# Twelve weight slots, an earlier second x block, TensorE fillers and transposed sums in the opening of a two-layer hybrid backbone

## The chip, the cores and the metric

The kernel runs on one core of one Trainium2 chip. The metric is the device time of one execution in microseconds (us). TensorE (PE) multiplies matrices, VectorE (DVE), ScalarE (ACT) and GpSimd (POOL) do the elementwise work, and SyncE (SP) issues most of the DMA transfers from one queue, in order. Every engine works through its own queue in order and waits on semaphores for the others.

## The reference, cut to what matters

There are 1024 latent tokens and 256 context tokens of width 1024 and two layers. Each layer first makes six vectors of modulation from the conditioning, one set for the latent and one for the context tokens, and normalises:

```python
mod   = jax.nn.silu(c)     @ w_mod[l] + b_mod[l]      # (1, 3072): shift, scale, gate
mod_c = jax.nn.silu(c_ctx) @ w_mod[l] + b_mod[l]
h  = rms_norm(x, norm_g[l]) * (1.0 + scale)   + shift
hc = rms_norm(y, norm_g[l]) * (1.0 + scale_c) + shift_c
pl, pc = split_cols(h @ w_in[l]), split_cols(hc @ w_in[l])
o  = concat(attention(pl, pc), gated_delta_net(pl, pc), rg_lru(pl, pc)) @ w_out[l]
x  = x + gate * o
```

The three mixers read the same projection. The output is a last RMSNorm of x.

## The kernel before

Data is held transposed, 128 features by tokens. The tokens come in three blocks: A and B are the two halves of the latent tokens (512 each) and C the context (256). A normalised block h has eight parts d = 0 to 7 of 128 features each. The product with w_in is done in 34 tiles of 128 output columns; every tile does 24 matmuls for each block, since every operand is split into a high and a low part in fp32r (hi·hi, hi·lo, lo·hi for each d). The weights of a tile are loaded to "raw", rounded by ACT to "whi" (L841), and DVE makes "wlo" (L846).

The order of every engine's queue is not written by hand. A planner (class `Driver`) runs threads that yield operations with an estimated cost, and picks the one with the least start time plus priority; the priorities (`PR` and, for the second layer, `PR1`), the order of the tiles (`ORDER`, `ORDER1`) and some penalties are tables of numbers. So a change of one estimate can move instructions everywhere.

The opening, up to the third tile, runs in this way:

- Small constants are loaded by SP. Then `x_load` (L807) loads block A of x in eight parts, and `mod_load` (L635) the modulation weights: 4 chunks of 4 loads of 512 KB, in the order of chunks 0, 2, 1, 3. Chunks 0 and 2 hold shift and scale of d = 0 to 3, chunks 1 and 3 those of d = 4 to 7. The weights go to four slots "modw" of region X and to a buffer "sys" of region Y that takes two; a slot is free again when TensorE has used it. Blocks B and C of x are loaded after chunk 3.
- `mod_thread` (L658) multiplies a chunk with the vector silu(c) (tile "sc"), four matmuls side by side in 32 columns of the array each. ACT copies the sums out (L679), four small matmuls with the constant "sel2" add the four strips and transpose them (`fin`), and DVE adds the bias (L687) to modT; after a scale chunk it makes scA (L694).
- `stats` (L704) squares the parts (ACT L717), adds them up on DVE and POOL (L711), sums over partitions by a matmul with "ones", and makes the factor rs by two ACT steps (L733, L735). `norm_h` (L738) then multiplies each part by rs (L754), waits for the modulation of its half, scales and shifts it (L779), rounds it on ACT (L781) and makes the low part (L759, on DVE or POOL). After every four parts TensorE multiplies them with "wba" (`gates`); ACT copies that out (L792), TensorE transposes it with "sel16", and DVE copies it to "ba" (L802).
- `inproj` runs the first two tiles part by part, as the parts of h come; only when both are complete for A, B and C does it start the third tile.

Later in layer 0 an attention tile holds one of two locks from its start until its rotary step is done, and the table "rope" of that step is loaded after the DeltaNet inverses. The modulation of the gates and of layer 1 (eight more chunks, with the same `fin`) is made beside the attention.

Of the kernel before, what the change touches and what calls it, by code (L numbers as in the profile page):

```python
# [25 lines left out]
GROUPS = ((2, 3, 4, 5), (6, 7, 8, 9), (0, 1))  # L26

# [194 lines left out]
class Driver:  # L222


    def __init__(self):
# [7 lines left out]
        self.PR = {"att": -2.4, "att_k": -1.32, "att_q": -12.72, "atth": 0.74, "ba": 1.17, "evac": 0.39,  # L233
                   "gchain": 0.89, "gdn_q": -1.49, "gdn_v": 0.21, "gfin": -3.27, "gprep": 0.9, "gside": 1.09,
                   "inproj": 1.19, "inv": 1.02, "lru_x": -0.06, "lru_z": -2.13, "modlate": -1.36, "modload":
                   -14.53, "norm": -1.22, "normA": -8.86, "normB": -12.46, "normC": -3.27, "oproj": 0.33,
                   "osplit": -1.07, "prep": -1.73, "ptev": -0.13, "resid": -0.33, "rope": -1.03, "score": -0.15,
                   "wprep": -1.16, "z": -0.5}
        self.ops, self.late = [], False
        self.PR1 = {"att": -1.6, "att_k": -11.15, "att_q": -0.84, "atth": 0.05, "ba": -0.18, "evac": 0.37,  # L240
                    "gchain": 1.49, "gdn_q": -4.86, "gdn_v": 0.29, "gfin": -0.21, "gprep": 0.77, "gside": 0.4,
                    "inproj": 0.8, "inv": 0.24, "lru_x": -0.55, "lru_z": -0.49, "normA": 1.08, "normB": -1.62,
                    "normC": 12.1, "oproj": -1.07, "osplit": -0.26, "prep": -2.77, "ptev": -10.13, "resid":
                    -16.91, "rope": 3.42, "score": -0.66, "wprep": 1.03, "z": -0.87}
        self.margin, self.setpen, self.tilepen = 2.83, 1.1, 0.27
        self.cap = {"pe": 0.54, "dve": 0.3, "act": 0.26, "pool": 0.41}
# [209 lines left out]
def layout(inp):  # L456
# [57 lines left out]
    s2 = np.zeros((128, 2), np.float32)  # L514
    for j in range(4):
        for i in range(2):
            s2[32 * j + i, i] = 1.0
    A["sel2"] = s2
# [10 lines left out]
class Build:  # L529
# [1752 lines left out]
```

## Time and profile before

| | us |
|---|---|
| median of 3 runs | 2031.7 (2027.27 to 2031.89) |
| profiled execution, its own time | 2025.07 |
| its span | 2023.4 |
| TensorE busy in the span | 1927.2 (95%) |
| mean granted TensorE clock | 0.977 of full speed |

The profile's page gives for each engine the busy time, and in a band of 40 slices the busy tenths. TensorE is busy nearly everywhere; the exceptions are the first two slices, the end, and a few places in between. Matmuls are pipelined and their ends are modelled, so "busy" is not the same as "at its peak". The granted clock (PEclk) is 1.00 at 2.4 GHz and 0.50 at 1.2 GHz.

### The profile page before, as it was taken

The numbers are of one execution on the slowest core, as the hardware profiler recorded it, in microseconds if no ns is written. First come the engines' busy times: TensorE is split into PE (matmuls) and PEld (weight loads), VectorE is DVE, ScalarE is ACT, GpSimd is POOL, SyncE is SP. The second block draws the span as 40 slices with busy tenths as digits, with TensorE's granted clock in tenths as the row PEclk, the third lists the DMA queues.
The fourth block names the chain that finished last, engine by engine and source line by source line (L and its number), as shares of the span: only waits on it lengthen the run. The fifth ranks groups of instructions, "written<-read, shape, count | busy, mean of one in ns | idle before, by whom it ended". The sixth has DMA issues, their size and how long they took to land.

```text
span 2023.4 us, 34895 instructions
## 1 busy us (share of the span) xinstructions
PE 1927.2 (95%) x13014; PEld 1538.9 (76%) x13014; DVE 1321.9 (65%) x2556; ACT 1061.3 (52%) x1895; POOL 424.3 (21%) x604
## 2 busy tenths in 40 slices
PE   5899999999999999999999999999998999999997
PEld 2578888877888876777888688877776898776785
DVE  4767777898744356685533768969898444777433
ACT  3477676567333245465422577765667332566432
POOL 1402020000145522100331211110000676100132
PEclk8899999999999889999999999999999999899998
DMA  8037562325487868564633046563343888534643
GB/s 296 25 108 206 154 190 81 100 71 165 142 282 251 266 228 267 171 196 148 224 125 128 34 132 194 163 174 83 86 165 131 270 254 270 195 95 138 204 148 123
DMA packets 311738, 338.01 MB, mean 167 GB/s; under 512 B 63136, under 2 KB 220432, under 8 KB 311568
## 3 DMA queue, kind: packets, MB, share of 16 engines
q1 hardware_dynamic: 291696, 321.10, 51.1%
q10 hardware_dynamic: 19872, 14.68, 2.2%
q8 instruction: 102, 1.67, 0.4%
q14 instruction: 68, 0.56, 0.1%
HBM read 235.58 MB, written 94.87 MB: 163 GB/s over the span
## 4 chain that ended last, share of the span: by engine, by line
PE 65%; DVE 14%; ACT 8%; DMA 7%; issue 4%; SPq 1%; POOL 1%; ACTq 0%; DVEq 0%; POOLq 0%
PE psum L568 61%; PE psum L2017 3%; DVE regy L1317 3%; DVE regy L779 1%; DVE regy L577 1%; ACT regx L1950 1%; DVE regy L754 1%; DMA regy<-in_wmod_dram 1%; DVE wlo L846 1%; DVE regy L1479 1%; ACT whi L841 1%; DMA regy<-regy 1%; DVE regy L1324 1%; DVE regy L1481 1%; PE psum L1199 1%
## 5 line engine op out<-in xcount | busy, mean ns | idle before, releaser
L568 PE MATMUL psum<-regx,whi 128*128 128x512 f32 (+1 forms) x3328 | 953.2, 372 | 18.9 <-ACT regy L1224 8.9
L568 PEld LDWEIGHTS psum<-regx,whi 128*128 128x128 f32 x3328 | 592.2, 189 | 145.5 <-issue 19.6
L568 PE MATMUL psum<-regx,wlo 128*128 128x512 f32 (+1 forms) x1664 | 610.6, 367 | 0.4 <-DVE wlo L846 0.4
L568 PEld LDWEIGHTS psum<-regx,wlo 128*128 128x128 f32 x1664 | 314.8, 189 | 53.6 <-DVE wlo L846 0.8
L568 PE MATMUL psum<-regy,regy 128*128 128x128 f32 (+4 forms) x4064 | 318.9, 265 | 6.9 <-DMA regy<-regy 4.7
L568 PEld LDWEIGHTS psum<-regy,regy 128*128 128x128 f32 (+2 forms) x4064 | 265.7, 148 | 53.6 <-issue 28.1
L841 ACT ACTIVATE whi<-raw 128x1024 fp32r<-128x1024 f32 (+1 forms) x132 | 125.7, 953 | 171.8 <-PE psum L568 159.6
L568 PE MATMUL psum<-regx,regx 128*64 128x256 f32 (+2 forms) x1184 | 195.4, 368 | 5.3 <-DVE regx L1916 1.6
L846 DVE TENSOR_TENSOR wlo<-raw,whi 128x1024 fp32r<-128x1024 f32 (+1 forms) x100 | 117.5, 1176 | 69.0 <-ACT whi L841 67.2
L568 PE MATMUL psum<-regy,whi 128*128 128x512 f32 (+1 forms) x576 | 157.9, 360 | 4.5 <-DVE regy L2090 2.3
L568 PEld LDWEIGHTS psum<-regx,regx 128*128 128x128 f32 (+1 forms) x1184 | 116.0, 166 | 56.1 <-issue 26.3
L846 POOL TENSOR_TENSOR wlo<-raw,whi 128x768 fp32r<-128x768 f32 x32 | 59.1, 1847 | 347.6 <-ACT whi L841 309.4
L1224 ACT ACTIVATE regy<-psum 128x512 f32<-128x512 f32 (+1 forms) x124 | 64.9, 525 | 123.2 <-PE psum L568 110.0
L2160 DVE SCALAR_TENSOR_TENSOR regy<-psum,modT,regy 128x512 f32<-128x512 f32 (+1 forms) x40 | 27.8, 696 | 148.2 <-PE psum L568 148.2
L568 PEld LDWEIGHTS psum<-regy,whi 128*128 128x128 f32 x576 | 102.1, 189 | 24.9 <-DVE regy L2090 3.7
L1950 ACT ACTIVATE regx<-regx,regx 128x640 f32<-128x640 f32 (+2 forms) x144 | 109.0, 759 | 22.5 <-DVE regx L1942 16.6
L1317 DVE SCALAR_TENSOR_TENSOR regy<-regy,gcv,regy 128x1282 f32<-128x1282 f32 x72 | 111.6, 1552 | 13.1 <-ACT regy L1313 11.8
L2051 ACT ACTIVATE regx<-psum 128x512 f32<-128x512 f32 x114 | 65.1, 591 | 94.6 <-PE psum L2017 83.2
L1630 POOL TENSOR_TENSOR regy<-regy,regy 128x512 f32<-128x512 f32 x76 | 97.4, 1304 | 70.9 <-DMA regy<-kqd 53.7
L1673 POOL TENSOR_SCALAR_AFFINE_SELECT regy<-regy 128x128 f32<-128x128 f32 (+1 forms) x240 | 71.3, 334 | 187.3 <-DMA regy<-XXd 96.4
L568 PE MATMUL psum<-regy,wlo 128*128 128x512 f32 (+1 forms) x288 | 102.5, 356 | 0.0
L2017 PE MATMUL psum<-ident,regx 128*128 128x128 f32 x640 | 95.4, 283 | 1.9 <-ACT regx L1950 1.3
(193 smaller groups left out, 2559.3 us busy)
## 6 DMA issues: line engine op xcount, KB each, us to landing
raw<-in_win_dram SPq DMA_DIRECT2D x68, 512.0 KB
raw<-in_wout_dram SPq DMA_DIRECT2D x64, 384.0 KB
regy<-kqd SPq DMA_DIRECT2D x76, 256.0 KB
raw<-in_wmod_dram SPq DMA_DIRECT2D x32, 512.0 KB
regy<-od SPq DMA_DIRECT2D x24, 512.0 KB
regy<-egd SPq DMA_DIRECT2D x40, 256.0 KB
regy<-ktd SPq DMA_DIRECT2D x40, 256.0 KB
regy<-vtd SPq DMA_DIRECT2D x40, 256.0 KB
```

The source lines that it names most:

```text
L568: self.nc.tensor.matmul(out, lhsT, rhs, start=start, stop=stop, skip_group_check=True)
L577: return (e, c_pool(n) if e == "pool" else c_dve(n), lambda: eng.tensor_tensor(out, a, b, op), R, Wr)
L841: yield ("act", c_act(n), lambda: nc.scalar.activation(hi.t[:, :n], raw.t[:, :n], AF.Copy), [raw], [hi])
L846: (nc.gpsimd if e == "pool" else nc.vector).tensor_tensor(lo.t[:, :n], raw.t[:, :n], hi.t[:, :n].bitcast(F32), OP.subtract)
L1224: yield ("act", c_act(n), lambda: nc.scalar.activation(dst.t[:m, o:o + n], ps.t[:m, :n], AF.Copy), [ps], [dst])
L1317: yield ("dve", c_dve(GW), lambda: nc.vector.scalar_tensor_tensor(y.t[:, :GW], xp.t[:, k:k + GW], w[:, k:k + 1], y.t[:, :GW], OP.mult, OP. ...
L1630: yield ("pool", c_pool(512), lambda: nc.gpsimd.tensor_tensor(b.t, b.t, ga.t, OP.mult), [ga, b], [b])
L1673: nc.gpsimd.affine_select(out[:, :, 32 * b:32 * b + 32], src, [[0, 4], [0, 32]], OP.is_ge, 0.0, base=32 * b + 31 if up else -32 * b, chann ...
L1950: yield ("act:e", c_act(nk, 1) + .1, lambda: nc.scalar.activation(P, P, AF.Exp, bias=one(0, h), scale=-1.0, accum_out=one(8, h)), [Ps[j], ...
L2017: nc.tensor.transpose(pt.t[:, 128 * j:128 * j + 128], Ps[j].t[:, 128 * i:128 * i + 128], self.I.t)
L2051: yield ("act", c_act(512), lambda: nc.scalar.activation(PT.t, pt.t, AF.Copy), [pt], [PT])
L2160: yield ("dve", c_dve(n), lambda: nc.vector.scalar_tensor_tensor(xn.t[:, :n], ps.t[:, :n], g.t[:, 16 + dt, who:who + 1], xn.t[:, :n], OP.m ...
```

## The change

- The region X gets twelve slots "modw" instead of four, below the first h block.
- `x_load` puts block B after chunk 2, and `mod_load` puts chunk 1 after block B; block C follows chunk 3 as before.
- `fin` transposes the copied-out sums with four matmuls against the identity, and DVE adds the four strips by one `tensor_reduce`; the bias is then added in a second step.
- A thread `warm` yields up to 400 matmuls of 128x128 by the identity, at a low priority, from block A's load until the last part of h of block C. 33 are in the program.
- Seven loads of constants go from SP to ACT, and one (sel2) is gone.
- The zeroing of the padding of a convolution tile in layer 0 becomes a thread of its own.
- The planner's estimate of a load depends on the length of its contiguous pieces. `PR`, `PR1`, `ORDER`, `ORDER1` and the penalties have new numbers.

```diff
+def piece(ap):
+    r = 1
+    for st, n in reversed(list(ap.ap)[1:]):
+        if st != r and n > 1:
+            break
+        r *= n
+    return 4 * r
...
-        self.PR = {"att": -2.4, "att_k": -1.32, "att_q": -12.72, "atth": 0.74, "ba": 1.17, "evac": 0.39,
+        self.PR = {"att": -2.3, "att_k": -6.36, "att_q": -21.71, "atth": 0.51, "ba": 1.13, "evac": -0.31,
...
     def load(self, dst, src, buf, nbytes, q="sp", R=()):
+        nbytes *= 0.69 + 150.0 / min(piece(dst), piece(src))
...
-        nc.sync.dma_start(self.fg.t, A["fg"])
-        self.s2 = self.one(cp, "sel2", [128, 2])
-        nc.sync.dma_start(self.s2.t, A["sel2"])
+        nc.scalar.dma_start(self.fg.t, A["fg"])
...
             def fin():
                 for k in range(4):
-                    self.mm(p2.t[:, 2 * k:2 * k + 2], ev.t[:, 128 * k:128 * k + 128], self.s2.t, True, True)
-            yield ("pe", 0.89, fin, [ev, self.s2], [p2])
+                    nc.tensor.transpose(p2.t[:, 128 * k:128 * k + 128], ev.t[:, 128 * k:128 * k + 128], self.I.t)
+            yield ("pe", 0.45, fin, [ev], [p2])
+            yield ("dve", 0.15, lambda: nc.vector.tensor_reduce(
+                mt.t[:, 4 * cc:4 * cc + 4, :], p2.t.rearrange("p (a j b) -> p a b j", a=4, j=4)[:, :, 0:2, :],
+                mybir.AxisListType.X, OP.add), [p2], [mt])
...
-            if blk == "A":
-                yield ("wait", self.event(box, 0, 3, 3))
+            if blk != "C":
+                yield ("wait", self.event(box, 0, 2 if blk == "A" else 3, 3))
...
                 if conv and dst.fresh:
                     dst.fresh = False
-                    yield ("pool", 0.5, lambda: self.pads(dst.t, C["last"]), [], [dst])
+                    if l:
+                        yield ("pool", 0.5, lambda: self.pads(dst.t, True), [], [dst])
+                    else:
+                        pad = drv.spawn(self.pad0(dst), -20.0, "pad")
...
+    def pad0(self, dst):
+        m = Buf(None)
+        m.w, m.r = dst.w, dst.r
+        yield ("pool", 0.5, lambda: self.pads(dst.t, False), [], [m])
+        dst.w = max(dst.w, m.w)
...
-    ORDER = ("gdn_k0", "gdn_q1", "gdn_q0", "gdn_k1", "gdn_k3", "gdn_v0", "gdn_q2", "gdn_k2", "gdn_z2", "gdn_q3",
+    ORDER = ("gdn_k0", "gdn_q0", "gdn_k1", "gdn_q1", "gdn_v3", "lru_x3", "gdn_k2", "gdn_q2", "lru_x0", "lru_z3",
...
-        X.at = 16896
-        self.modp = Zone(X).slots("modw", 4, [1024])
+        X.at = 8704
+        self.modp = Zone(X).slots("modw", 12, [1024])
...
+    def warm(self):
+        yield ("wait", self.xev["A"])
+        ps = yield ("alloc", self.ps1)
+        for i in range(400):
+            if self.ev(0, "h", "C", 7).set:
+                break
+            yield ("pe", c_pe(128, "f"), lambda: self.mm(ps.t[:, :128], self.I.t, self.I.t, True, True), [], [ps])
+        ps.free()
...
-        drv.spawn(self.mod_load(0, [self.modp, self.modp, z["sys"]], (0, 2, 1, 3), box, {0: self.xev["A"]}), 0.1, "modload", self.ev("mod"))
+        drv.spawn(self.mod_load(0, [self.modp, self.modp, z["sys"]], (0, 2, 1, 3), box, {0: self.xev["A"], 1: self.xev["B"]}), 0.1, "modload", self.ev("mod"))
...
+        drv.spawn(self.warm(), 0.0, "warm")
```

In SP's queue of the opening, before: the last two modulation weights are followed by blocks B (xT) and C (ctxT).

```order
L572 DMA regx_179<-in_wmod_dram 128x1024
L572 DMA regx_180<-in_wmod_dram 128x1024
L572 DMA regy_190<-in_xT_dram 128x512 x2
L572 DMA regy_191<-in_xT_dram 128x512 x2
L572 DMA regy_192<-in_xT_dram 128x512 x2
L572 DMA regy_193<-in_xT_dram 128x512 x2
L572 DMA regy_196<-in_ctxT_dram 128x256 x5
```

In the same queue after the change, the end of block B and the start of chunk 1; the eight parts of block B alternate with small parameters.

```order
L578 DMA regy_197<-in_xT_dram 128x512
L578 DMA gn_104<-in_gnorm_dram 128x1
L578 DMA regy_197<-in_xT_dram 128x512
L578 DMA sink_106<-in_sink_dram 128x8
L578 DMA regy_198<-in_xT_dram 128x512
L578 DMA wba_157<-in_wba_dram 128x256
L578 DMA regy_198<-in_xT_dram 128x512
L578 DMA regx_181<-in_wmod_dram 128x1024
L578 DMA regx_182<-in_wmod_dram 128x1024
L578 DMA ab_103<-in_alog_dram 128x8
L578 DMA regy_210<-in_wmod_dram 128x1024 x2
```

Block B now stands ahead of chunks 1 and 3, eight small loads are mixed into it, and only the two weights in regy_210 still wait for TensorE.

In TensorE's queue, before: the second half of chunk 3 (tile sc) stands behind the first matmuls of the first projection tile (whi, wlo).

```order
L568 MATMUL psum_81<-regx_178,sc_63_157 32x512
L568 MATMUL psum_80<-regx_181,whi_173 128x512 x2
L568 MATMUL psum_80<-regx_181,wlo_175 128x512
L568 MATMUL psum_80<-regx_181,whi_173 128x512
L568 MATMUL psum_80<-regx_181,whi_173 128x512 [waits Pool_49]
L568 MATMUL psum_80<-regx_181,wlo_175 128x512
```

After: chunk 3, its transposes, the sum of squares of block B (ones), and only then the first projection tile.

```order
L573 MATMUL psum_84<-regx_186,sc_62_155 32x512 [waits DMAHW4_49]
L573 MATMUL psum_84<-regx_186,sc_62_155 32x512
L689 MATMUL psum_85<-ident_114,regy_203 128x128 [waits Activation_49]
L689 MATMUL psum_85<-ident_114,regy_203 128x128 x3
L573 MATMUL psum_86<-regy_199,ones_119 128x512 [waits DVE_49]
L573 MATMUL psum_82<-regx_187,whi_171 128x512 x2
L573 MATMUL psum_82<-regx_187,wlo_173 128x512
```

The projection moved behind chunk 3, and the 33 fillers stand elsewhere: 22 at the head of the queue, 6 between chunks 2 and 1, 4 before block C's tiles and 1 before the third tile.

In DVE's queue after the change, the scale and shift of block A's last parts and the first parts of block B, around the copy to "ba":

```order
L787 TENSOR_SCALAR regy_194<-regy_194,scA_153,modT_151 128x512 x2
L762 TENSOR_TENSOR regy_195<-regy_195,regy_204 128x512 [waits DMAHW5_49,Activation_49]
L787 TENSOR_SCALAR regy_195<-regy_195,scA_153,modT_151 128x512 [waits DVE_49]
L762 TENSOR_TENSOR regy_195<-regy_195,regy_204 128x512 [waits DMAHW7_49]
L810 COPY ba_158<-psum_83 128x64 [waits PE_49]
L787 TENSOR_SCALAR regy_195<-regy_195,scA_153,modT_151 128x512 [waits DVE_49]
```

The copy waits for TensorE and stands ahead of nearly all of block B's work, whose sums of squares are now ahead of this piece of the queue.

## Rows read from the trace of the kernel before

**Rows 1.** The page's head: busy time of the engines, share of the span, instructions; one of its groups

```profile
span 2023.4 us, 34895 instructions
PE 1927.2 (95%) x13014; PEld 1538.9 (76%) x13014; DVE 1321.9 (65%) x2556; ACT 1061.3 (52%) x1895; POOL 424.3 (21%) x604
...
L568 PE MATMUL psum<-regy,regy 128*128 128x128 f32 (+4 forms) x4064 | 318.9, 265 | 6.9 <-DMA regy<-regy 4.7
```

**Rows 2.** Busy time by stretch: length, PE, PEld, DVE, ACT, POOL, PEclk, DMA share, GB/s

```profile
0.00:102.00 102.00, 70.33 (x313) 37.46 (x314) 61.16 (x109) 40.65 (x80) 31.70 (x40) 0.87 0.45 159
102.00:565.00 463.00, 457.26 (x2606) 378.42 (x2604) 367.77 (x516) 302.03 (x473) 36.04 (x72) 1.00 0.47 139
690.00:725.00 35.00, 29.60 (x297) 25.42 (x296) 12.09 (x53) 8.35 (x23) 17.09 (x24) 0.61 0.88 302
950.00:975.00 25.00, 25.00 (x112) 20.56 (x111) 10.40 (x14) 10.08 (x13) 6.81 (x4) 1.00 0.76 247
```

**Rows 3.** TensorE in time: start, length, line, operands, count, wait; the third tile starts

```profile
102.20 0.63 PE L568 MATMUL psum<-regx,whi 128*128 128x512 f32 x2
```

**Rows 4.** SP's queue in time: first issue, first weights, modulation weights, blocks B and C

```profile
0.80 0.39 SPq L2216 DMA_DIRECT2D bm<-in_bmod_dram  x1
5.03 0.43 SPq L572 DMA_DIRECT2D raw<-in_win_dram  x1
11.50 2.31 SPq L572 DMA_DIRECT2D regx<-in_wmod_dram  x4
37.73 0.80 SPq L572 DMA_DIRECT2D regx<-in_wmod_dram  x2
38.59 7.08 SPq L572 DMA_DIRECT2D regy<-in_xT_dram  x8
```

**Rows 5.** Busy time by short stretches of the opening, columns as in rows 2

```profile
0.00:46.00 46.00, 23.07 (x93) 7.73 (x94) 21.18 (x38) 15.05 (x22) 8.64 (x21) 0.85 0.82 286
20.00:22.00 2.00, 2.00 (x4) 0.50 (x2) 0.00 (x0) 0.00 (x0) 0.00 (x0) 1.00 1.03 420
22.00:28.00 6.00, 3.22 (x25) 1.28 (x24) 2.57 (x5) 1.80 (x3) 0.00 (x0) 1.00 0.61 164
46.00:48.00 2.00, 2.00 (x6) 1.61 (x5) 0.00 (x0) 0.63 (x1) 0.00 (x0) 0.50 1.05 399
```

**Rows 6.** The chain that ended last, in the opening: start, length, what

```profile
5.03 4.21 DMA raw<-in_win_dram
36.34 14.52 PE psum L568 x52
51.59 1.07 PE psum L568 x8
52.88 0.57 DVE scA L694
```

**Rows 7.** TensorE in time: a chunk's matmuls and projection at either clock

```profile
22.11 1.06 PE L568 MATMUL psum<-regx,sc 128*32 128x512 f32 x8
43.07 1.93 PE L568 MATMUL psum<-regx,sc 128*32 128x512 f32 x8
46.38 1.05 PE L568 MATMUL psum<-regx,whi 128*128 128x512 f32 x2
```

**Rows 8.** DVE's groups from 53.5 to 102 us: count, busy, mean ns, idle before

```profile
L779 DVE TENSOR_SCALAR regy<-regy,scA,modT 128x512 f32<-128x512 f32 x12 | 10.9, 916 | 0.3
L711 DVE TENSOR_TENSOR regy<-regy,regy 128x512 f32<-128x512 f32 x4 | 5.1, 1276 | 2.2 <-ACT regy L717 2.0
```

**Rows 9.** SP's queue around the rotary table and the first stores of query tiles

```profile
480.81 0.40 SPq L572 DMA_DIRECT2D regy<-in_rope_dram  x1
494.10 3.19 SPq L1185 DMA_DIRECT2D qstd<-regy  x6
```

**Rows 10.** DVE's busy time by stretch of the opening, columns as in rows 2

```profile
53.50:80.00 26.50, 20.28 (x71) 10.72 (x70) 21.07 (x29) 14.07 (x29) 13.46 (x10) 0.81 0.05 20
80.00:104.00 24.00, 21.87 (x128) 15.51 (x128) 19.71 (x42) 10.71 (x26) 8.31 (x9) 1.00 0.00 1
```

More of the change, by code (lines that the diff above doesn't have):

```diff
@@ L239, in __init__ @@
-        self.ops, self.late = [], False
[L240 to L244, printed above, removed]
@@ L245, in __init__ @@
-        self.margin, self.setpen, self.tilepen = 2.83, 1.1, 0.27
-        self.cap = {"pe": 0.54, "dve": 0.3, "act": 0.26, "pool": 0.41}
+        self.PR = {"att": -2.3, "att_k": -6.36, "att_q": -21.71, "atth": 0.51, "ba": 1.13, "evac": -0.31,
+                   "gchain": 0.85, "gdn_q": -1.82, "gdn_v": 0.25, "gfin": -7.48, "gprep": 0.63, "gside": 1.07,
+                   "inproj": 1.3, "inv": 0.64, "lru_x": -0.21, "lru_z": -4.98, "modlate": -1.32, "modload":
+                   -8.75, "norm": -2.44, "normA": -14.23, "normB": -14.07, "normC": -1.83, "nrmB": 0.31, "nrmC":
+                   1.3, "oproj": 0.41, "osplit": -0.53, "prep": -1.4, "ptev": -2.9, "resid": -1.16, "rope":
+                   -1.64, "score": -0.16, "warm": 5.67, "wprep": -10.04, "z": -4.66}
@@ new lines, in __init__ @@
+        self.ops, self.late = [], False
+        self.PR1 = {"att": -1.75, "att_k": -20.38, "att_q": -2.2, "atth": -0.89, "ba": 0.83, "evac": 0.36,
+                    "gchain": 1.05, "gdn_q": -8.12, "gdn_v": 0.41, "gfin": 2.91, "gprep": -0.76, "gside": 0.13,
+                    "inproj": 0.8, "inv": 0.23, "lru_x": -0.54, "lru_z": -0.41, "normA": 1.22, "normB": 1.72,
+                    "normC": 16.65, "oproj": -0.75, "osplit": 0.06, "prep": -3.26, "ptev": -7.21, "resid":
+                    -12.87, "rope": 11.69, "score": -1.85, "wprep": 0.02, "z": -0.71}
@@ L247, in __init__ @@
+        self.margin, self.setpen, self.tilepen = 2.96, 1.13, 0.41
+        self.cap = {"pe": 0.55, "dve": 0.34, "act": 0.35, "pool": 0.41}
         self.port, self.tile, self.sync, self.dry = dict(dve=0.0, pool=0.0), "", {}, False
@@ L513, in layout @@
     A["sel"] = sel
[L514 to L518, printed above, removed]
     s16 = np.zeros((128, 16), np.float32)
@@ L594, in consts @@
         self.mask = self.one(cp, "mask", [128, 3, 128], BF)
-        stage = self.X.tile(16896)
+        stage = self.X.tile(8704)
         mf = stage[:, 512:896].rearrange("p (a b) -> p a b", a=3)
@@ L620, in consts @@
         f = stage[:, 256:264]
-        nc.sync.dma_start(f, A["sel"])
+        nc.scalar.dma_start(f, A["sel"])
         nc.vector.tensor_copy(self.sel.t, f)
@@ L925, in begin @@
             yield ("wait", boxes[t]["ev"])
-            dst = None
+            dst = pad = None
             conv = kind in ("gdn_k", "gdn_q", "gdn_v", "lru_x")
@@ L2215, in run @@
             for l in range(2):
-                nc.sync.dma_start(self.bm[l].t, A["bmod"][l])
-                nc.sync.dma_start(self.ngt[l].t, A["ng"][l])
+                nc.scalar.dma_start(self.bm[l].t, A["bmod"][l])
+                nc.scalar.dma_start(self.ngt[l].t, A["ng"][l])
             self.consts(cp)
```

29 lines of the change are left out of this document (12 added, 17 removed).

## The prediction

> **What bounds the kernel now.** I read the page's head first: TensorE is busy for 1927.2 of 2023.4 us [rows 1], so an edit pays only where TensorE idles or runs at its lower clock. The table by stretch says where that is: in the first 102 us it is busy for 70.3 us at a clock of 0.87, in the 463 us after that it idles for 5.7 us at full clock [rows 2]. Beyond the opening one place stands out, 690 to 725 us, with 5.4 us idle and a clock of 0.61 [rows 2]. The mark that counts for the opening is the start of the third projection tile, at 102.2 us [rows 3]: the first two wait for all parts of h, and behind them TensorE is nearly saturated. What moves that mark forward moves everything after it by as much, unless the new order loses it elsewhere.
>
> The chain of waits shows what sets the mark: first DMA, then 14.5 us of TensorE at 36.3 to 50.9, then the sums and transposes of chunk 3 and scA at 53.45 [rows 6], and from there to 102 DVE, busy for 40.8 of 50.5 us [rows 10].
>
> **The change part by part.** *Head of SP's queue.* Its first issue is at 0.80 and the first weights go out at 5.03, behind nine small loads [rows 4]. Only one of the nine stays, so the weights go out at about 1.3. But the third load after them waits, by the new queue, on the same DMA counter as the weights, and those took 4.2 us to land [rows 6]. So block A and the modulation weights (first issue now 11.5) start earlier by between 0 and 3.8 us; I take 2.2, nearer to the upper end, since fewer transfers share the DMA meanwhile. ACT's seven issues cost it 3 us at 0.43 us each [rows 4], while it waits for its first data anyway: nothing.
>
> *Twelve slots.* From 22 to 28 us the DMA moved 164 GB/s, against 420 just before [rows 5]: 0.98 MB, which at 420 would take 2.3 us. Here weights wait for slots and small loads fill the queue. I count 3.7 us gained by the end of chunk 2 (from 0, if the small loads alone did it, to 3.7). Chunk 2 is then there about 6 us earlier.
>
> *Block B ahead of chunks 1 and 3.* 2.1 MB at 399 GB/s [rows 5] are 5.3 us before chunk 3. Eight small loads between its parts double the issues to 16, at 0.47 us from one to the next 7.5 us [rows 4]; I take 7.4. Before, the last weight load was out by 38.6 [rows 4] and 13.2 MB had been moved by 46 us (286 GB/s [rows 5]), block B's first parts among them. After, chunk 3 ends when 14.0 MB are there: 46 + 0.8/0.4 - 2.2 - 3.7 + 2.1 (issue) = 44.2; counted forward, with 2.8 MB there at 13 us and 0.4 MB/us from then on, it is 41. I take 43, bounds 41 to 47.
>
> *Chunk 3 to scA.* Before, TensorE took up chunk 3 late: its queue had projection matmuls at the lower clock ahead (1.05 us for two, against 0.63 at 102 us [rows 3, 7]; a chunk half 1.93 instead of 1.06 us [rows 7]). These now stand behind. From the last weights to scA I count 1.2 us of matmuls, 0.6 for ACT, 0.9 for four transposes (between 0.45 and 1.07, the old small matmuls [rows 6]), 0.5 for DVE's reduction, bias and scA, which has no row for the reduction (the nearest, scA itself, took 0.57 [rows 6]), and 0.3 of semaphores: 3.5 us. scA comes at **46.5 instead of 53.45: 7 us** (bounds 3 and 9).
>
> *scA to the third tile.* This took 48.7 us. DVE's busy time in it was about 40.8 us [rows 10], of which the sums of squares of block B, 5.1 us with 2.2 idle ahead of them [rows 8], are now done before. That leaves 35.7 us and DVE's waits. Two of these I can walk through. The copy to "ba" now stands ahead of block B [the order of DVE's queue above]; it waits for gates and transposes behind TensorE's ones, 24 projection matmuls of block A and the gates. TensorE starts that at 45.7 with about 4 us at the lower clock: 45.7 + 2.1 + 9 x 0.45 + 15 x 0.22 + 2 = 57.2 at the latest (0.22 us is 25 us by 112 [rows 2], 0.45 twice that), 55.5 where the steps overlap. DVE is ready at 50.5. So it waits some 5 us, and for block B's copy about 5 again. Block C's part adds its chain. Bounds: 36 us if DVE never waits, 48.7 if nothing is won; the walk gives 43.5, and I take 43.7, **5 us less** than before.
>
> *Fillers.* 22 run at the head while TensorE has nothing to do (it starts at 17.5 before), 6 between chunks while it waits for data, 5 near the end. No row shows one alone; the float32 matmuls of 128 columns are two records of 0.27 us each [rows 1], which overlap. So the 22 take at most 12 us, and the last 5 at most 2.7, of which I take 1, inside the walk. What they do for the clock: chunk matmuls alone did not keep it up before, it reads 0.50 at 46 us [rows 5], and the chunk half at 43 took nearly twice that at 22 [rows 7]. The fillers stand 15 us and more ahead of the moment that counts, so I give them nothing.
>
> *Rest of the program.* The projection, attention and output have the same instructions; only their order is new. In the attention's start (690 to 725) 5.4 us idle and 11.5 us by the clock were lost [rows 2]. In the new queue 24 projection matmuls (5 us) stand ahead of that place instead of 6, which covers part; between -10 and +10, I take **2 us gained** there and nothing elsewhere. The 8 reductions and 32 transposes of the later chunks lie beside other work.
>
> Sum: 7 + 5 + 2 = 14 us, since 46.5 + 43.7 puts the third tile at 90.2, 12 us ahead, and 2 come later. The profiled execution, 2025.1, becomes 2011; it ran 6.6 us below the median of the runs shown, 0.3%. Taken off the median: **2018 us**.
>
> **The rivals.** *The opening gives much more.* If TensorE holds the full clock from chunk 3 on, the copies don't hold DVE, and the stretch falls to its 36 us: 7 + 13 + 2, 2010 us. For it: from 46 us on TensorE has 24 matmuls ready without a wait, which it lacked before. Against: the clock was low at just this kind of work [rows 5, 7].
>
> *The clock falls again.* After scA the old run had a clock of 0.81 over 26.5 us [rows 10], since TensorE waited for parts of h. If the new one waits as often, each wait holds DVE too, by the copies. That costs 8 us more than I count: 2026 us. The Trainium skill ("TensorE: Matmul & The Clock Gate", HAM oscillation) says the same in general: a TensorE that waits for DMA between bursts drops to the lower clock and starts every burst there. By it the fillers at the head are wasted. This trace agrees in the row at 46 us, though the row at 20 us reads the full clock [rows 5] after an idle start.
>
> *The opening doesn't move.* If the loads are held by the counter at the head and by the issues between the parts of block B, chunk 3 ends at 47, scA gains 3 and the stretch after it nothing, as its waits take what the sums gave: 2029 us.
>
> *Slower.* In layer 0 the new order starts a query tile as the 16th and another as the 24th; they hold both attention locks until their rotary step, and the 27th tile, a query too, can't start before. The table is loaded behind the 28th weight load instead of the 27th. Before, 16.5 us passed from that load to the end of the first query tile's stores [rows 9], and this was hidden. If it is exposed along with one tile (13.4 us: 48 matmuls of 0.22 and 24 of half that [rows 2]), 30 us are lost and 14 won: about 2047 us. It decides for slower from an idle of 20 us on. Against: other work (DeltaNet, LRU gates) filled such waits before; from 102 to 565 us TensorE idled only for 5.7 us [rows 2].
>
> **How the numbers follow.** About 0.3% (6 us) is what a measurement of this kernel can tell from no change. The forecast (2010 to 2024) has a chance of 0.45, much more gain 0.18, the falling clock 0.17, an opening that doesn't move 0.12, slower 0.08. Faster by over 0.3%, below 2025.6: 0.44 + 0.18 + 0.09 = 0.71. Within 0.3%: 0.01 + 0.08 + 0.11 = 0.20. Slower: 0.09. The range reaches from 2003, which is the first rival with the upper end at the head (1.6 more) and half of the bound for the rest (5 more), to 2031, which takes in the opening that doesn't move.
>
> **What would show it.** The third tile's first matmul at about 90 us (82 in the first rival, 96 or more in the next two); scA of chunk 3 at 46.5; no dip of the DMA rate between 20 and 40 us; DVE idle ahead of the two copies to "ba"; a clock of 0.50 from 40 to 50 us. The stretch from the third tile to the end should be as long as before, 1921 us, or 2 us shorter. The prediction is wrong if that stretch changes by more than 8 us, or if chunk 3's weights land after 47 us.

## The result, and the profile after

The changed kernel takes 2008.6 us (median, 2008.1 to 2012.6), the kernel before 2031.8 (2027.3 to 2034.4) beside it: a ratio of 0.9893, 95% interval 0.9871 to 0.9914. The forecast was 2018 us in a range of 2003 to 2031. So the sign and the range hold, but the gain is 23 us where the sum said 14. The profiled execution after took 2008.4 us, next to its median; that of the kernel before took 2025.1, and of 45 executions of the kernel before that ran beside the experiments (medians 2030.5, 2028.1 and 2027.9) three were shorter. This matters below: a gain of 16.7 us between the two traces is 23 between the medians taken side by side, and 19 against the lowest of the three later medians of the kernel before. Each kernel below was run beside the kernel before, not beside the changed one; where that matters they are compared by their ratios to it.

The head of the page, then busy time by stretch of the kernel after (length, PE, PEld, DVE, ACT, POOL with counts, granted clock, DMA share, GB/s):

```profile
span 2006.7 us, 34974 instructions
PE 1917.6 (96%) x13032; PEld 1538.9 (77%) x13032; DVE 1314.7 (66%) x2568; ACT 1057.1 (53%) x1895; POOL 422.7 (21%) x604
```

```profile
0.00:46.00 46.00, 25.54 (x138) 12.73 (x138) 26.91 (x43) 19.15 (x30) 14.54 (x24) 0.78 0.89 312
28.00:34.00 6.00, 1.74 (x16) 1.54 (x14) 5.42 (x11) 3.42 (x7) 1.58 (x2) 0.83 0.80 216
46.00:48.00 2.00, 1.57 (x8) 0.14 (x4) 1.79 (x3) 0.25 (x1) 0.00 (x0) 1.00 1.06 369
53.50:80.00 26.50, 25.33 (x131) 18.14 (x129) 17.18 (x27) 13.56 (x28) 12.38 (x10) 1.00 0.06 20
682.00:717.00 35.00, 31.95 (x377) 28.30 (x376) 17.13 (x46) 10.08 (x23) 15.74 (x32) 0.90 0.96 306
```

Against the rows of before: the clock at 46 us is 1.00 instead of 0.50 [rows 5], from 53.5 to 80 it is 1.00 instead of 0.81 [rows 10], and at the attention's start (8 us earlier in the new kernel) 0.90 instead of 0.61 [rows 2]. The DMA has moved 312 GB/s by 46 us instead of 286 [rows 5], yet there is still a dip, to 216 GB/s from 28 to 34 us.

The chain that ended last, in the opening (start, length, what), where [rows 6] stands for the kernel before:

```profile
31.22 6.36 DMA regx<-in_wmod_dram
37.59 9.02 DMA regx<-in_wmod_dram
46.65 1.08 PE psum L573 x4
47.75 0.61 ACT regy L683
48.40 0.66 PE psum L689 x4
49.06 26.84 PE psum L573 x132
```

The 14.5 us of TensorE ahead of the sums are gone from the chain. It is DMA until 46.61, when chunk 3's last weights land, and then 3 us to scA. TensorE in time (start, length, line, operands, count): the fillers at the head, the third tile, and the first and the last score matmul of layer 0's attention:

```profile
1.43 6.72 PE L573 MATMUL psum<-ident 128*128 128x128 f32 x44 [1.43 <-POOL ident masks.py:199]
...
93.89 0.73 PE L573 MATMUL psum<-regx,whi 128*128 128x512 f32 x2
...
733.29 0.65 PE L573 MATMUL psum<-regx,regx 128*64 128x256 f32 x4
...
931.61 0.65 PE L573 MATMUL psum<-regx,regx 128*64 128x256 f32 x4 [1.02 <-ACT regx L2068]
```

DVE in time, after: scA of chunk 3, the two long copies to "ba" of the opening, and the first one of layer 1:

```profile
49.52 0.17 DVE L702 SCALAR_TENSOR_TENSOR scA<-modT,ngt 128x8 f32<-128x8 f32 x1
...
58.07 0.21 DVE L810 COPY ba<-psum 128x64 f32<-128x64 f32 x1
...
74.44 0.23 DVE L810 COPY ba<-psum 128x64 f32<-128x64 f32 x1 [4.25 <-PE psum L573]
...
1006.12 0.23 DVE L810 COPY ba<-psum 128x64 f32<-128x64 f32 x1 [3.52 <-PE psum L573]
```

The third tile starts at 93.9 instead of 102.2 us [rows 3]: 8.3 us, where 12 were forecast. From there to the end it takes 1912.8 instead of 1921.2 us: 8.4, where 2 were forecast. So of the two terms one was too large and the other much too small. The same marks in the kernel before, TensorE first, then DVE:

```profile
741.90 0.87 PE L568 MATMUL psum<-regx,regx 128*64 128x256 f32 x6
...
947.98 0.87 PE L568 MATMUL psum<-regx,regx 128*64 128x256 f32 x6
```

```profile
1026.48 0.23 DVE L802 COPY ba<-psum 128x64 f32<-128x64 f32 x1 [3.54 <-PE psum L568]
```

From the third tile to the first score matmul both take the same (639.7 before, 639.4 after). Layer 0's attention, from first to last score matmul (the last one starts 0.7 us behind the start of its row before, and 0.3 after), falls from 206.8 to 198.6 us, and the way from there to layer 1's gates from 77.8 to 74.2.

DVE from the end of scA to the third tile (columns as in the rows by stretch), before and then after:

```profile
53.45:102.20 48.75, 40.79 (x193) 25.38 (x193) 39.45 (x69) 23.00 (x53) 21.78 (x18) 0.89 0.03 11
```

```profile
49.70:93.90 44.20, 40.78 (x218) 29.65 (x216) 29.78 (x65) 20.75 (x49) 17.42 (x16) 0.96 0.06 15
```

DVE is busy for 29.8 instead of 39.5 us and idles for 14.4 instead of 9.3.

### The profile page after: what moved, and what is told of

It is laid out like the page before. It is cut to its first block, busy times and chain, and to the rows that moved or that the text cites. A ratio compares the mean times of both kernels' runs of the same rounds, so it can differ in the third digit from the quotient of the medians.

```text
span 2006.7 us, 34974 instructions
## 1 busy us (share of the span) xinstructions
PE 1917.6 (96%) x13032; PEld 1538.9 (77%) x13032; DVE 1314.7 (66%) x2568; ACT 1057.1 (53%) x1895; POOL 422.7 (21%) x604
## 3 DMA queue, kind: packets, MB, share of 16 engines
q1 hardware_dynamic: 290544, 321.05, 51.5%
## 4 chain that ended last, share of the span: by engine, by line
PE 73%; DVE 9%; DMA 8%; ACT 5%; issue 2%; POOL 1%; SPq 1%; ACTq 0%; DVEq 0%; POOLq 0%
PE psum L573 68%; PE psum L2034 3%; DVE regy L1334 2%; DMA regx<-in_wmod_dram 1%; SPq L578 1%; DMA regx<-vatd 1%; PE psum L1216 1%; DMA raw<-in_win_dram 1%; DMA regy<-kqd 1%; DVE regy L762 1%; ACT whi L849 1%; DVE regy L1341 1%; DMA regy<-XXd 1%; DMA regx<-rd 1%; DVE regy L787 1%
## 5 line engine op out<-in xcount | busy, mean ns | idle before, releaser
L573 PEld LDWEIGHTS psum<-regx,regx 128*64 128x64 f32 (+1 forms) x1184 | 114.3, 163 | 64.2 <-issue 26.8
L1435 POOL TENSOR_SCALAR_AFFINE_SELECT regy<-regy 128x512 f32<-128x512 f32 (+1 forms) x48 | 30.9, 646 | 330.3 <-ACT regy L1430 282.3
```

What stands on the lines that cost most here:

```text
L573: self.nc.tensor.matmul(out, lhsT, rhs, start=start, stop=stop, skip_group_check=True)
L1435: yield ("pool", c_pool1(n), lambda: nc.gpsimd.affine_select(m3, s3, [[0, nch], [-1, 128]], OP.is_gt, 0.0, base=0, channel_multiplier=1), ...
```

## Experiments on the opening

Kernels named "a_..." are the changed kernel with one edit, "b_..." the kernel before with one. Unless said otherwise the edit leaves every other instruction at its place in every queue. The mark is again the start of the third tile (93.9 in the changed kernel, 102.2 before).

**Small loads behind chunk 3's weights.**

```diff
+    def emit(self, who, eng, fn):
+        if eng == "sp" and who == "params":
+            self.seen += 1
+            if self.nmod < 16 and self.seen > 2:
+                self.held = (self.held or []) + [fn]
+                return
+        fn()
...
-                fn()
+                self.emit(th.name, name, fn)
```

> The changed kernel with every instruction in its order, except that the small parameter loads that stand between the parts of block B in SP's queue (and two more ahead of them) are issued behind chunk 3's last weights. Theory: these issues set when chunk 3's weights land. From 28 to 34 us the DMA moves 193 to 243 GB/s against 420 at 18 to 20, while SP issues one load every 0.47 us, and half of them are of a few KB. Ten fewer issues bring chunk 1 and 3 forward by 4 to 5 us: weights of chunk 3 at 42 instead of 46.6, scA at 45 instead of 49.5, the third tile at 89.5 instead of 93.9, the time 2004. Rival: the work on block B (sums of squares on DVE from 39 to 48 us) or TensorE at the lower clock takes the place of the weights. Then the weights still land at 42, but scA comes 0 to 2 us earlier and the third tile starts at 92 to 94.

SP's queue in the changed kernel from 26 us on, a small load between each two parts of block B, and behind the weights those of the third tile and block C (start, length, queue, what, count):

```profile
26.51 0.43 SPq L578 DMA_DIRECT2D lb<-in_lbias_dram  x1
26.99 0.43 SPq L578 DMA_DIRECT2D regy<-in_xT_dram  x1
...
31.22 0.91 SPq L578 DMA_DIRECT2D regx<-in_wmod_dram  x2
...
34.23 3.70 SPq L578 DMA_DIRECT2D regx<-in_wmod_dram  x4
38.95 0.33 SPq L578 DMA_DIRECT2D raw<-in_win_dram  x1
39.33 9.00 SPq L578 DMA_DIRECT2D regy<-in_ctxT_dram  x8
```

With the edit: SP's queue, the DMA's stretch, and the third tile; then the stretch up to the landing of chunk 3's last weights with the edit (42.53) and in the changed kernel (46.61):

```profile
27.49 1.00 SPq L594 DMA_DIRECT2D regx<-in_wmod_dram  x2
...
30.16 2.22 SPq L594 DMA_DIRECT2D regx<-in_wmod_dram  x4
...
43.45 0.38 SPq L594 DMA_DIRECT2D raw<-in_win_dram  x1
43.87 4.37 SPq L594 DMA_DIRECT2D regy<-in_ctxT_dram  x8
```

```profile
28.00:34.00 6.00, 2.65 (x18) 1.95 (x20) 5.41 (x10) 3.42 (x7) 1.26 (x1) 0.96 1.04 407
```

```profile
89.80 0.74 PE L589 MATMUL psum<-regx,whi 128*128 128x512 f32 x2
```

```profile
0.00:42.53 42.53, 26.28 (x138) 12.78 (x138) 27.28 (x43) 19.05 (x30) 13.62 (x24) 0.88 0.89 327
```

```profile
0.00:46.61 46.61, 26.06 (x138) 12.73 (x138) 27.45 (x43) 19.15 (x30) 14.54 (x24) 0.78 0.89 313
```

The dip is gone (407 instead of 216 GB/s), chunk 1's first weights go out 3.7 us earlier, scA starts at 45.44 instead of 49.52, the mark is 4.1 us earlier. The median is 2000.5 us (ratio 0.986, 0.983 to 0.989; its interval overlaps that of the changed kernel). The theory's 89.5 was right. Nine small loads (0.5 to 24 KB, and one of 128 KB), each with its issue and its place among the loads in flight, stood ahead of the last weights; from 28 to 34 us the DMA moved 1.1 MB less with them (191 GB/s for 6 us). But the edit does a second thing that the theory doesn't name: the small loads now hold up the third tile's weights and block C, which go out 4.5 us later. When chunk 3's last weights land, 13.9 MB have been moved instead of 14.6 (the rates above by their times). By estimate these 0.7 MB are 1.7 us at 407 GB/s, so up to that much of the 4.1 us can be transfers that no longer run beside the weights. No run parts the two. Together they are the step between the forecast landing (43) and the measured one (46.6). The Trainium skill ("DMA: Bandwidth & Descriptors", Issuing engines are not separate DMA queues) calls the time that a sequencer takes to start a DMA usually small beside the DMA itself. Here one issue follows another after 0.47 us, and half a megabyte, the larger loads' size, takes 1.3 us at 407 GB/s: about a third, and not small where every other issue is a load of a few KB.

**No fillers.**

```diff
-            yield ("pe", c_pe(128, "f"), lambda: self.mm(ps.t[:, :128], self.I.t, self.I.t, True, True), [], [ps])
+            yield ("pe", c_pe(128, "f"), lambda: None, [], [ps])
```

> The changed kernel with every instruction in its order, but without the 33 fillers, whose results nobody reads. Theory (the prediction's): they do nothing on the path. Chunk 3 waits for its weights until 46.6 us with or without them, so the third tile starts at 93.9 us, give or take 1, and the time is 2008 us, give or take 4. Rival: they are what keeps the clock at 1.00 from 42 us on. Then the clock reads 0.50 again at 46 to 50 us without them, chunk 3's last matmuls and transposes take 1 to 2 us more and the first projection matmuls twice their time, and the third tile starts at 96 to 98.

The mark is 94.47, 0.6 later, and chunk 3's weights landed 0.6 us later too (47.19). The median is 2006.0 us (ratio 0.9879, 0.9859 to 0.9898). So they give nothing, as the prediction had it. Busy time without the fillers, and below it with them:

```profile
16.00:22.00 6.00, 5.11 (x18) 0.86 (x18) 2.33 (x4) 2.35 (x4) 0.58 (x7) 1.00 1.02 412
46.00:48.00 2.00, 1.77 (x8) 0.24 (x8) 1.75 (x3) 0.00 (x0) 0.00 (x0) 1.00 1.03 367
```

```profile
16.00:22.00 6.00, 6.00 (x18) 1.04 (x18) 1.94 (x3) 1.28 (x3) 0.21 (x7) 0.52 1.03 417
```

The two rows from 16 to 22 us look as if the 22 at the head lowered the clock: they run from 1.4 to 8.1 us, TensorE then idles for 7.8 us, and the row reads 0.52, against 1.00 where nothing ran before. The lengths of the matmuls say otherwise. TensorE's groups without the fillers, from 15 to 19.1 and from 23 to 26 us, and with them from 15 to 19.1 (count, busy, mean ns, idle before):

```profile
L573 PE MATMUL psum<-regx,sc 128*32 128x512 f32 x8 | 3.1, 1046 | 16.4 <-DMA regx<-in_wmod_dram 16.4
```

```profile
L573 PE MATMUL psum<-regx,sc 128*32 128x512 f32 x8 | 2.1, 604 | 0.2 <-DMA regx<-in_wmod_dram 0.2
```

```profile
L573 PE MATMUL psum<-regx,sc 128*32 128x512 f32 x8 | 3.1, 1057 | 7.8 <-DMA regx<-in_wmod_dram 7.8
```

The first matmuls of chunk 0 take 1.05 us each with and without the fillers, against 0.60 later: both start at the lower clock. Without fillers the trace has no clock record before 19.3 us, and the view counts a stretch without records as the full clock. At 46 us the clock is 1.00 either way.

**Old sums.**

```diff
-                    nc.tensor.transpose(p2.t[:, 128 * k:128 * k + 128], ev.t[:, 128 * k:128 * k + 128], self.I.t)
+                    self.mm(p2.t[:, 2 * k:2 * k + 2], ev.t[:, 128 * k:128 * k + 128], self.s16.t[:, :2], True, True)
...
-            yield ("dve", 0.15, lambda: nc.vector.tensor_reduce(
...
+            yield ("dve", 0.15, lambda: None, [p2], [mt])
...
```

> The changed kernel with every instruction in its order, but with the old sums: four matmuls with a column matrix in place of each four transposes, and no reduction on DVE. Theory: the new sums give nothing by themselves, since four transposes take 0.66 us at the full clock and the reduction 0.19, while the old matmuls took 0.45 at that clock. scA then comes 0.2 to 0.5 us earlier than in the changed kernel, and the third tile starts at 93.4 to 93.9; time 2008. Rival: the transposes are faster on the path, and the third tile starts 0.5 to 1 us later with the old sums.

The mark is 94.17 with weights that landed 0.2 us earlier (46.41), so the old sums are slower by 0.2 us up to scA and by 0.5 up to the mark, and the median is 2007.5 us (0.9884, 0.9863 to 0.9905). The rival had the sign: at the full clock the four small matmuls show as 1.05 us, the four transposes as 0.66, which is more than the reduction adds. It is too little to be seen in the time.

**Four slots.** From the moment at which all of h is complete, this kernel and the next follow the recorded order of the changed kernel (the edit for that is shown below). Ahead of it the planner is free, so other instructions of the opening move as well.

```diff
-        X.at = 8704
-        self.modp = Zone(X).slots("modw", 12, [1024])
+        X.at = 16896
+        self.modp = Zone(X).slots("modw", 4, [1024])
```

> The changed kernel with four slots for modulation weights instead of twelve; from the moment at which all of h is complete the order is that of the changed kernel. Theory: weights wait for slots, that is for TensorE's matmuls on the chunk before, and chunk 3's weights land at 49 to 51 instead of 46.6; the third tile starts at 97 to 98 instead of 93.9, the time is 2011 to 2013. Rival: while weights wait, block B and the small loads fill the queue, the bytes are the same, and the third tile starts within 1 us of 93.9.

Chunk 3's weights land at 49.9 (the chain shows their transfer from 42.55, 7.36 us), and the third tile starts at

```profile
98.92 0.73 PE L683 MATMUL psum<-regx,whi 128*128 128x512 f32 x2 [0.31 <-ACT whi L959]
```

5.0 us later than with twelve. The median is 2011.2 us (0.9912, 0.9897 to 0.9927). The 3.7 us that the prediction gave the slots are 3.3 at the landing; another 1.7 is lost behind it, most of it because TensorE takes up the last chunk at the lower clock (scA starts 4.2 instead of 2.9 us behind the landing; chunk 3's last four matmuls take 1.95 instead of 1.08 us).

**Block B behind chunks 1 and 3.**

```diff
-            if blk != "C":
-                yield ("wait", self.event(box, 0, 2 if blk == "A" else 3, 3))
+            if blk == "A":
+                yield ("wait", self.event(box, 0, 3, 3))
...
-        drv.spawn(self.mod_load(0, ... {0: self.xev["A"], 1: self.xev["B"]}), ...
+        drv.spawn(self.mod_load(0, ... {0: self.xev["A"]}), ...
```

> The changed kernel with block B of x loaded behind the weights of chunks 1 and 3 again; from the moment at which all of h is complete the order is that of the changed kernel. Theory (the prediction's two terms): scA comes earlier by the 2.1 MB that no longer stand ahead, 5 us and some issues, so at 42 to 44 instead of 49.5; but block B's sums of squares fall behind it again, and scA to the third tile takes 48 to 49 instead of 44.4 us. The third tile starts at 91 to 93, 1 to 3 us earlier than in the changed kernel: moving block B ahead was no gain. Rival: DVE's waits grow by more than these 5 us, as block B itself lands only at 50, and the third tile starts at 95 or later.

scA starts at 46.05, 3.5 us earlier than in the changed kernel, but from there the third tile takes 51.5 us, 7.1 more:

```profile
97.55 0.73 PE L683 MATMUL psum<-regx,whi 128*128 128x512 f32 x2 [0.32 <-ACT whi L959]
```

So by the mark moving block B ahead is worth 3.7 us, and the rival was right. In the time it can't be seen: 2005.7 us (0.9894, 0.9876 to 0.9913). In its trace the 3.7 us are made up by the first score matmul, which starts at 733.3 us in both; a second pair of traces would be needed to tell whether that is chance.

**Constants back on SP's queue.**

```diff
-                nc.scalar.dma_start(self.bm[l].t, A["bmod"][l])
-                nc.scalar.dma_start(self.ngt[l].t, A["ng"][l])
+                nc.sync.dma_start(self.bm[l].t, A["bmod"][l])
+                nc.sync.dma_start(self.ngt[l].t, A["ng"][l])
...
```

The other three of the seven loads (fg, sel16, sel) are moved back in the same way.

> The changed kernel with every instruction in its order, but with the seven small loads that it moved to ACT's queue back at the head of SP's. Theory: the modulation weights go out as late as before, at 11.5 instead of 9.1 us, everything up to chunk 3 moves by about 2.4 us (its weights land at 49), and the third tile starts at 96 instead of 93.9; time 2010. Rival: the loads are held by the landings of the eight ahead anyway (1.28 us from one issue to the next from 17 to 26 us), so the later start is made up, and the third tile starts within 0.7 us of 93.9.

The first modulation weights go out at 11.17 instead of 9.07 us, chunk 3's land at 48.36 instead of 46.61, the mark is 95.64: 1.75 us, and 2009.1 us (0.9903, 0.9879 to 0.9928). The later landing is the theory's, a little short of its 2.4.

## Experiments on the rest

**Old rest, new rest.** The planner's choices of either kernel were recorded. In the two hybrids the opening is planned as usual, and once all of h is complete the next operation is always the one that comes first in the record of the other kernel, whose tables are used too.

```diff
             best = None
+            if self.mark.set:
+                best = self.follow()
...
+    def follow(self):
+        th = min(self.threads, key=lambda x: self.rank.get((x.label, x.i), -1), default=None)
+        return th and (0.0, self.ready(th.eng, th.op[3], th.op[4]), th)
```

> The changed opening (without its fillers), and from the moment at which all of h is complete the order of the kernel before, instruction for instruction, with its tables. Theory: the two halves of the change add up. The opening brings the third tile from about 102 to 94 or 95 us; the rest is worth about 14 us in the median by the order of its instructions, and is not there here. The time is 2030.5 - 8 = 2022, and from the third tile to the end it takes 1921 to 1931 us as in the two traces of the kernel before. Rival: the later stages gain because of the opening (another phase of transfers and waits), whatever the order. Then it takes 1908 to 1914 us as in the changed kernel, and the time is 2008.

> The counterpart: the opening of the kernel before (four slots, block B last, old sums, constants on SP's queue), and from the moment at which all of h is complete the order of the changed kernel. Theory: the third tile starts at 100 to 103 us, and from there to the end it takes 1908 to 1914 us; the time is about 2016. Rival (the later stages gain because of the opening): 1921 us or more to the end, and a time of 2026 to 2031.

The old opening with the new rest takes 2018.4 us (ratio 0.9945, 0.9925 to 0.9966) with its third tile at 104.65 us: 2.5 us later than in the kernel before, and still 10 us faster. From the mark to the end its profile takes 1908.2 us. So against the kernel before the order of the rest alone is worth 12 us, or 14 by the mark of 100.2 us in the second trace of the old opening (b_fill700, below). The theory is right here: the gain is there without the new opening.

The new opening with the old rest takes 2027.0 us (0.9989, 0.9975 to 1.0003), and here I was wrong about the mark. The last scale and shift of h on DVE, and the third tile on TensorE:

```profile
89.64 0.41 DVE L899 TENSOR_SCALAR regy<-regy,scA,modT 128x256 f32<-128x256 f32 x1
```

```profile
105.16 0.63 PE L683 MATMUL psum<-regx,whi 128*128 128x512 f32 x2
```

h is complete as early as in the changed kernel (there the last one starts at 89.70), but the mark is 11 us later. With the old tables the planner put the gates' matmuls for blocks A and B ahead of the first projection matmul, so TensorE waited with DVE and had its projection still to do. The opening's 8.3 us thus need both: loads that bring h earlier, and an order of TensorE's queue that has the projection done by then. From its mark to the end this kernel takes 1917.0 us, which is outside the theory's 1921 to 1931 and the rival's 1908 to 1914. The two hybrids ran side by side and their third tiles start 0.5 us apart, so they give a second price for the order of the rest: 8.6 us between their medians, and 8.8 from mark to end. The order is thus worth 8 to 14 us.

**New layer 0, old layer 1.** The changed kernel's record until layer 0's last output weights are requested, then the record of before with its tables.

```diff
                 drv.late = True
+                drv.recorded(RECORDED_OLD)
```

> The changed kernel, instruction for instruction, until layer 0's last output weights are requested; from there the order of the kernel before, with its table for layer 1. Theory: of the 14 us that the new order is worth behind the opening, 12 lie in layer 0 (its attention takes 192 to 198 us from the first to the last score matmul instead of 203 to 207, the stretch from there to layer 1's first gates 74 to 77 instead of 79), and in layer 1 a shorter attention (129 instead of 135) is paid for by 4 us more ahead of it. So this kernel is 1 to 3 us slower than the changed one: 2010 to 2012, with 134 to 136 us for layer 1's attention and 599 to 606 from the gates to it. Rival: layer 1's order is worth 6 us or more, and the time is 2014 to 2018.

2006.9 us (0.9886, 0.9862 to 0.9911), which isn't slower than the changed kernel, and less than the theory's 2010 to 2012: the new order of layer 1 is worth nothing that can be seen, and the rival (6 us or more) falls. The traces say where the gain is instead. In each row the kernels of one order lie within 6 us of each other, whatever their opening (within 11 in the fourth, where b_fill700 has a drop of the clock that is shown below); times in us between the starts of the instructions named, for each from its own profile:

| from, to | old order (before, b_fill700, new_open_old_rest) | new order (after and eight kernels with its edits or old opening) | new layer 0, old layer 1 |
|---|---|---|---|
| third tile, first score matmul | 639.7, 638.4, 635.1 | 635.8 to 641.3 | 636.6 |
| first, last score matmul of layer 0 | 206.8, 207.8, 203.3 | 194.1 to 198.6 | 199.8 |
| last score matmul, layer 1's gates | 77.8, 78.0, 78.1 | 73.6 to 75.1 | 73.4 |
| first gates, layer 1's first score matmul | 718.0, 728.7, 722.3 | 726.0 to 730.4 | 723.3 |
| first, last score matmul of layer 1 | 136.3, 135.9, 135.5 | 128.5 to 130.3 | 135.6 |
| last score matmul, end | 142.6, 142.5, 142.7 | 142.2 to 143.3 | 142.9 |

Twelve us lie in layer 0's attention and the stage behind it (between the two hybrids 12.8, of which the new order gives back 5.0 ahead of the attention); in layer 1 the 6 us of a shorter attention are spent ahead of it.

**Fillers at the attention's start of the kernel before.** There the clock falls at 697 us, while TensorE waits 2.57 us for a copy that stands behind ACT's own loads.

```diff
             def fin():
+                if l == 0 and cc == 4:
+                    for _ in range(9):
+                        self.mm(p2.t[:, :128], self.I.t, self.I.t, True, True)
```

> The kernel before, with nine extra matmuls ahead of the sums of the first late modulation chunk, so that TensorE works through its 2.6 us of waiting at 697 to 700 us. Nobody reads what they compute. Theory: the 8 us that the changed kernel gains beyond the opening are the clock at the attention's start in layer 0, which reads 0.50 from 697 to 727 us in the kernel before and falls there because TensorE idles. Kept busy, it stays at 1.00, and the kernel before becomes 8 to 12 us faster, about 2021. Rival: the transfers around it (the chain shows 3.8 and 4.9 us of them) set the pace, and it gains under 3 us. Second rival: the clock falls anyway a few us later, at the two waits of 709 to 711 us, and the gain is 3 to 6 us.

2027.0 us (0.9983, 0.9965 to 1.0000): 3.5 us, within the second rival and barely apart from nothing. In its trace, one of the longer executions (span 2031.5), the place itself is better, and another one is worse (below it the last of these rows for the kernel before):

```profile
0.00:102.00 102.00, 68.05 (x319) 37.35 (x320) 62.23 (x110) 42.72 (x82) 31.65 (x40) 0.93 0.45 159
690.00:725.00 35.00, 31.46 (x331) 26.80 (x331) 14.08 (x59) 10.82 (x30) 15.55 (x23) 0.76 0.90 305
1165.00:1579.00 414.00, 396.69 (x2101) 315.78 (x2094) 337.69 (x467) 277.42 (x427) 32.90 (x64) 0.98 0.47 142
```

```profile
1165.00:1579.00 414.00, 396.56 (x2155) 316.89 (x2152) 339.67 (x472) 279.51 (x431) 32.29 (x64) 1.00 0.49 144
```

From 690 to 725 us it loses 3.5 us by idling and 7.6 by the clock (31.46 x 0.24), 11 instead of 17 [rows 2]; the clock still falls at 697, is back at 700, and falls again at 707. In the ten kernels with the new layer 0 the same place, read in steps of 5 us over the 55 us that begin 585 us behind the mark, loses 6 to 11 us, in the three with the old one 11 to 19. But this place lies ahead of the first score matmul, and the stretch up to there takes as long in either order (first row of the table). What is lost here could count in the twelve us only as work that slips past the first score matmul, and b_fill700 speaks against much of that: its loss there is 11 instead of 19 us, its attention is as long as before (207.8), and its median gains 3.5 us at most. So the runs show that the twelve us belong to the new order of layer 0; what in that order saves them stays open.

**Both edits that help.** Small loads behind chunk 3, no fillers.

> The two edits that cost nothing or gained, together: the changed kernel with the small loads behind chunk 3's weights and without the fillers. Theory: the third tile starts at 89 to 90.5 us as with the small loads alone, and the time is 1999 to 2003. Rival: without fillers TensorE is idle for longer ahead of chunk 3, its clock is 0.50 when the weights land earlier, and the third tile starts at 91 or later.

The third tile starts at 88.39 us, scA at 44.03, and the time is 1999.6 us (0.9862, 0.9835 to 0.9888). With the small loads alone it was 2000.5. By their ratios both are 6 to 7 us faster than the changed kernel (0.9860 and 0.9862 against 0.9893), of which the mark explains 4 to 5.5. Their intervals overlap that of the changed kernel, so the mark is the surer sign. This kernel has the lowest median of the study.

## Why the prediction was right, and where it wasn't

- **Head of the queue**, 2.2 us: the weights went out 2.4 us earlier [rows 4], and putting the loads back cost 1.75. Right.
- **Twelve slots**, 3.7 us: 3.3 at the landing, 5.0 at the mark. Right at the landing, but it left out that TensorE took the late chunk at the lower clock.
- **Block B ahead**, 7.4 us lost for chunk 3: undoing it brought scA only 3.5 us forward. The rest of the 7.4 was the small loads' part: they stay ahead of chunk 3 when block B goes.
- **Chunk 3's weights at 43**: they landed at 46.6, near the upper bound of 47. This is the step that failed in the opening. I had 16 issues at 0.47 us in the sum but then took the DMA as nearly full; it fell to 216 GB/s from 28 to 34 us. I also let chunk 3 end when 14.0 MB are there; 14.6 were, since the third tile's weights and block C had gone out too. Taking the small loads out of the way changed both and gave 4.1 us back.
- **Chunk 3 to scA**, 3.5 us: 3.1, from 46.61 to 49.69. Right.
- **scA to the third tile**, 43.7 us: 44.2. That the sum fits is luck: it had 35.7 us of work on DVE and 8 of waits, and the trace has 29.8 and 14.4. The sums of squares of block B are gone from the stretch as foreseen. The 40.8 us that I started from run on to 104 us [rows 10] and are 39.5 up to the third tile, and most of the rest is that DVE's other instructions there were shorter (20 scales and shifts 13.8 instead of 15.5 us, 16 multiplications by rs 9.6 instead of 10.7), and no run shows why. Of the two waits of 5 us ahead of the copies to "ba" one is 4.25 us and the other isn't there; 3.7 us of waits ahead of block B's and C's multiplications stand in its place.
- **Fillers**, nothing: right.
- **Rest of the program**, 2 us: 8.4 between the two traces, 8 to 14 by the hybrids. This is the term that was mis-sized. It looked at the attention's start alone and put "nothing elsewhere", while the attention itself and the stage behind it took 12 us less. By the prediction's own sentence (wrong if that stretch changes by more than 8 us) this part was wrong. That the total came within the range rests on two errors of opposite sign: 12 us forecast and 8.3 measured up to the third tile, 2 and 8.4 behind it.

Of the rivals, the first had its premise and not its gain: the clock is 1.00 from 44 to 80 us, but scA to the third tile took 44 us and not 36, since DVE idled for 14.4 of them. The second, a clock that falls again behind scA, didn't happen (1.00 from 53.5 to 80 us). The Trainium skill ("TensorE: Matmul & The Clock Gate", HAM oscillation) has a TensorE that waits for DMA between bursts start each burst at the lower clock; the trace agrees for the waits of 7.8 us at the head and of 7.9 us ahead of chunk 1; chunk 3 has only short waits for weights (0.23 us each without the fillers), and there the clock stays at 1.00. The row at 20 us, which the prediction set against it, is no counterexample: in the kernel before, too, the eight matmuls that start at 17.5 us take 1.06 us each where they take 0.60 later, in a stretch without clock records. The third rival, an opening that doesn't move, was close in its first half (weights at 46.6 where it had 47, scA 3.8 us earlier where it had 3), but the stretch behind scA gave 4.5 us more. The attention locks of the fourth rival cost nothing: the first score matmul comes as long behind the mark as before.

## What to carry to other kernels

Count the issues of a queue as time wherever small loads stand among large ones: moving nine of them out of the way, and with them what stood behind, gave 4 us on a path that was all transfer. When a change moves the order of a whole program, an edit's place says little about where its gain is; marks at stage boundaries, and a run that keeps the old order behind one of them, tell the parts apart. And one profiled execution is one draw: here it was near the fast edge of the old kernel's runs.

## What the runs showed of the hardware

The same program gives another clock in another execution. The kernel before and b_fill700 have the same instructions up to 697 us, but in the first 102 us the clock read 0.87 in one and 0.93 in the other, and the third tile started at 102.2 and 100.2 us. From 1165 to 1579 us one lost nothing by the clock and the other 2% of 397 us, 8 us. Executions of one kernel lie 4 to 20 us apart (1993.6 to 2013.5 for a_smalls_late); such drops of the clock are the largest difference that I found between traces of one order.

The program's first matmuls on chunk 0 ran at the lower clock in all 13 traces, with fillers ahead of them and without: the first eight take 3.05 to 3.12 us together, where eight at the full clock take 1.06. In the traces without fillers the view by stretches reads 1.00 there, for want of a record (the first begins at 18 to 22 us). A clock of 1.00 at a program's start is worth checking against the lengths of the matmuls.
